# Moving the causal mask of the forgetting heads from TensorE to VectorE

## The chip, the cores and the metric

The kernel runs on one core of a Trainium2 chip. The metric is the device time of one execution in microseconds (us). The engines are called by their short names: PE is TensorE (matrix products), DVE is VectorE, ACT is ScalarE, POOL is GpSimd, and SP is SyncE, which issues most DMAs.

## The reference

One decoder layer for 512 positions of width 1024. Its first half runs two kinds of causal attention side by side on the same input, 8 heads of width 64 each, and merges them; its second half is a gated MLP with a short convolution. Only the first half matters here.

```
# forgetting attention (FoX), 8 heads
cum = cumsum(log_sigmoid(f + b_forget))
logits = q k^T / 8 + cum[t] - cum[s];  logits[s > t] = -inf
y = softmax(logits) v
# stick-breaking attention, 8 heads
z = q k^T / 8
a[t,s] = sigmoid(z[t,s]) * prod_{s<j<t} (1 - sigmoid(z[t,j]))   for s < t, else 0
y = a v
```

## The kernel before

All products keep fp32 accuracy by splitting each operand into a high part that PE takes exactly (type fp32r) and a low rest, so that one product becomes three: high with high, high with low, low with high (lines 134 to 136). Weights arrive by DMA as `raw` tiles of 128 x 1024; ACT makes the high part `wh` (line 183) and DVE the low part `wl` (line 93), a few tiles ahead of their use.

The program begins with `first_mm` (line 307), which runs the first seven column groups of the input projection and the forget logits over eight slices of the model width, while their weights and the modulation stream in. The tiles of this part lie in a pool `early`. When it is closed, the pool `att` is laid over the same memory, and a tile of `att` can be written only once the early tiles below it have been read. `att` holds the tiles that the change touches: `s2t` and `m2t`, four each, the operands of a second score product. POOL fills parts of them (lines 345 to 349).

Then come 16 heads, the 8 stick-breaking ones (`br == 1`) first and the 8 forgetting ones (`br == 0`) after. A head goes through three stages: `stage_a` computes the scores of four blocks of 128 rows into three PSUM banks and turns them into weights `pt`; `stage_b` transposes `pt` on PE and splits it; `stage_c` multiplies with the values. Between the stages of successive heads, `fill(n)` issues n products of other projections. The order on each engine is not exactly that of the text: a planner in the framework orders the instructions of PE, DVE, ACT and POOL by their place in the text and by when it expects their inputs; only SP's order is written by hand.

In `stage_a`, `scores(i)` makes two products for block i. The first (line 482) has 128 rows: high and low parts of q (`s1`) against the high part of k, twice (`m1`). The second (line 483) has 68 rows: 64 rows of high q against the low part of k, and four rows that bring in the cumulated forget logits of a forgetting head (high and low part, for t and for s). For a stick-breaking head `s2` is `s1` itself, and rows 64 to 67 of `m2` are zero. For a forgetting head `decay_rows` copies the four rows by DMA from POOL's queue. `mask(i)` (line 488) adds a triangle of -1e30 to the diagonal block of a forgetting head by a product of a bf16 identity with a bf16 triangle. Then DVE takes the negated row maximum from PSUM (line 504), and ACT the exponential with that as bias and the row sum beside it (line 505); DVE scales by the reciprocal (lines 506 and 510).

Of the kernel before, what the change touches and what calls it, by code (L numbers as in the profile page):

```python
# [8 lines left out]
F32 = mybir.dt.float32  # L9
F32R = mybir.dt.float32r  # L10
BF16 = mybir.dt.bfloat16
AF = mybir.ActivationFunctionType
ALU = mybir.AluOpType
AX = mybir.AxisListType
PSUM = bass.MemoryType.PSUM

P = 128
# [11 lines left out]
NEG = -1.0e30  # L29
# [22 lines left out]
def layer_kernel(ctx: ExitStack, tc: tile.TileContext, out, xT, x, cT, crow, wa0, wa1, bcol, bgt, w1, wct, wv, bf,  # L52
# [3 lines left out]
    V, S, G, PE = nc.vector, nc.scalar, nc.gpsimd, nc.tensor  # L56
# [15 lines left out]
    def nm(s):  # L72
        cnt[0] += 1
        return f"{s}_{cnt[0]}"

    def bank():
        return pp.tile([P, 512], F32, name=nm("ps"), tag="ps")
# [5 lines left out]
    def const(shape, dt, s):  # L83
        return cons.tile(shape, dt, name=s, tag=s)

    def fl(ap):
        return ap.bitcast(F32)
# [8 lines left out]
    def preset(shape, dt, s):  # L96
        return pre.tile(shape, dt, name=s, tag=s)
# [10 lines left out]
    ident = const([P, P], F32, "ident")  # L108
# [5 lines left out]
    make_identity(nc, ident)  # L114
    onesr = const([P, P], F32R, "onesr")
    V.tensor_copy(onesr, ones)
    identb = preset([P, P], BF16, "identb")
    V.tensor_copy(identb, ident)
    zerob = preset([P, P], BF16, "zerob")
    G.memset(zerob, 0.0)  # L120
    mska = preset([P, P], BF16, "mska")
    G.affine_select(mska, zerob, pattern=[[-1, P]], compare_op=ALU.is_ge, fill=NEG, base=0, channel_multiplier=1)
    dg = preset([P, 512], F32, "dg")
    G.memset(dg[:, 0:384], 0.0)
    G.tensor_copy(dg[:, 384:512], ident)
# [4 lines left out]
    def z(dt, s, shape=(P, 512)):  # L130
        return zp.tile(list(shape), dt, name=nm(s), tag="z", bufs=NZ)
# [14 lines left out]
    def weights(i, ahead=AHEAD):  # L146
        while state["load"] < min(len(items), i + depth[0]):
            it = items[state["load"]]
            if it[2] == 512:
                late = state.get("late")  # L150
                it[3] = late.tile([P, 512], F32, name=nm("rl"), tag="rl", bufs=4) if late else z(F32, "rs")
            else:
                it[3] = stg.tile([P, 1024], F32, name=nm("raw"), tag="raw", bufs=LOADS)
            c = 0
            for src in it[0] if isinstance(it[0], list) else [it[0]]:
                w = src.shape[-1]
                d = nc.sync.dma_start(it[3][:, c : c + w], src)
                c += w
                if depth[0] < LOADS and state["load"] >= depth[0]:
                    paced(d, reads[state["load"] - depth[0]])  # L160
            if len(it) > 5:
                G.dma_start(it[3], it[5], accum_op=ALU.add)  # L162
            state["load"] += 1
            while state["proc"] <= state["load"] - depth[0]:
                process()
        while state["proc"] < min(len(items), i + 1 + ahead):
            process()
        return items[i][4]
# [25 lines left out]
    for e in range(2):  # L194
        c = slice(e * 512, (e + 1) * 512)
# [139 lines left out]
    att = st2.enter_context(tc.tile_pool(name="att", bufs=1, reuse_waits="tile"))  # L335

    OFS = ((0, 0), (2, 0), (0, 128), (1, 0))
    SEG = (((0, 128), (128, 512)), ((0, 512),), ((0, 256),))
    ptc = [[att.tile([P, 512], F32R, name=f"ptc{i}{e}", tag=f"ptc{i}{e}") for e in range(2)] for i in range(2)]
    for e in ptc:  # L340
        for t in e:
            G.memset(fl(t[:, 0:128]), 0.0)
    s2t = [att.tile([68, 512], F32R, name=f"s2_{i}", tag=f"s2_{i}") for i in range(4)]
    m2t = [att.tile([68, 512], F32R, name=f"m2_{i}", tag=f"m2_{i}") for i in range(4)]
    for t in s2t:
        G.memset(fl(t[64:68, :]), 1.0)
        G.memset(fl(t[64:66, :]), -1.0)
    for t in m2t:
        G.memset(fl(t[64:68, :]), 0.0)
    chi = att.tile([NH, 2, 512], F32R, name="chi", tag="chi")  # L350


# [22 lines left out]
    def decay_rows(h):  # L375
        n = slot_free(idx(0, h))
        if h < 4:
            G.memset(fl(m2t[n][64:68, :]), 1.0)
        G.dma_start(s2t[n][66:68, :], chi[h : h + 1, :, :])
        G.dma_start(m2t[n][64:66, :], chi[h : h + 1, :, :])  # L380
# [9 lines left out]
    def idx(br, h):  # L390
        return h if br == 1 else NH + h
# [82 lines left out]
    def stage_a(br, h):  # L474
        d = hd[(br, h)]
        bk = [bank(), bank(), bank()]

        def scores(i):
            b, o = OFS[i]
            w = max(256, (i + 1) * P)  # L480
            tb = slice(i * P, (i + 1) * P)
            PE.matmul(bk[b][:, o : o + w], d["s1"][:, tb], d["m1"][:, 0:w], start=True, stop=False)
            PE.matmul(bk[b][:, o : o + w], d["s2"][0:68, tb], d["m2"][0:68, 0:w], start=False, stop=br == 1)  # L483

        def mask(i):
            b, o = OFS[i]
            if br == 0:
                PE.matmul(bk[b][:, o + i * P : o + i * P + P], identb, mska, start=False, stop=True)

        scores(0)  # L490
        mask(0)
        scores(2)
        scores(1)
        scores(3)
        mask(2)
        mask(1)
        mask(3)
        pt = [z(F32, "pt"), z(F32, "pt"), z(F32, "pt")]
        if br == 0:
            sm = att.tile([P, 12], F32, name=nm("sm"), tag="sm", bufs=3)  # L500
            for i in (0, 2, 1, 3):
                b, o = OFS[i]
                c = slice(o, o + (i + 1) * P)
                V.tensor_reduce(sm[:, i : i + 1], bk[b][:, c], AX.X, ALU.max, negate=True)
                S.activation(pt[b][:, c], bk[b][:, c], AF.Exp, bias=sm[:, i : i + 1], accum_out=sm[:, 4 + i : 5 + i])
            V.reciprocal(sm[:, 8:12], sm[:, 4:8])
            for i in (0, 2, 1, 3):
                b, o = OFS[i]
                c = slice(o, o + (i + 1) * P)
                V.tensor_scalar_mul(pt[b][:, c], pt[b][:, c], sm[:, 8 + i : 9 + i])  # L510
        else:
            for b in (0, 2, 1):
                w = SEG[b][-1][1]
                om = z(F32, "om")
                S.activation(om[:, 0:w], bk[b][:, 0:w], AF.Sigmoid, scale=-1.0)
                d["last"] = S.activation(pt[b][:, 0:w], bk[b][:, 0:w], AF.Sigmoid)
                G.memset(pt[b][:, SEG[b][0][1] - 1 : w : 384], 0.0)
                for s, e in SEG[b]:
                    d0 = om[:, s + 1 : e][:, ::-1]
                    V.tensor_tensor_scan(d0, d0, dg[:, 513 - (e - s) : 512][:, ::-1], 0.0, ALU.mult, ALU.max)  # L520
                    G.tensor_tensor(pt[b][:, s : e - 1], pt[b][:, s : e - 1], om[:, s + 1 : e], ALU.mult)  # L521
        d["pt"] = pt
        scored.add(idx(br, h))
        if br == 0 and h + 4 < NH:
            decay_rows(h + 4)
        if br == 1 and h >= 4 and gated:
            decay_rows(h - 4)
# [272 lines left out]
    forget_evac()  # L800
    fill(12)
    stage_a(1, 0)
    for j in range(1, NG):
        gate_after(1, j)(grp[2 + j])
    fill(18)
    stage_a(1, 1)
    fill(48)
    stage_b(1, 0)
# [3 lines left out]
    for n, (b, h) in enumerate(heads):  # L812
        f1, f2, f3 = FILL[n // 8]
        if n + 2 < 16:
            if n == 6:
                fill_to(marks["vf"])
                forget(items[vfi[0]][5])
            if n % 2 == 0:
                fill_to(marks[(n // 2 + 1, "k")])
            last = hd[heads[n + 1]].get("last")  # L820
            stage_a(*heads[n + 2])
        fill(f1)
        if n + 1 < 16:
            stage_b(*heads[n + 1])
        fill(f2)
        if n == 0:
            fill_to(marks["v1"])
            fill(9)
        stage_c(b, h)
        if n == 7:  # L830
            lim[0] = marks["y0"]
        if n == 15:
            lim[0] = len(stream)
        fill(f3)
# [158 lines left out]
    for n in range(2 * FT):  # L993
# [7 lines left out]
        if n in (23, 27):  # L1001
            t = t13[(23, 27).index(n)][:, 0:512]
# [5 lines left out]
        if n in (28, 31, 32, 35):  # L1008
            k = (28, 31, 32, 35).index(n)
            w = wdp[FP - 1][:, k * 512 : (k + 1) * 512]  # L1010
# [115 lines left out]
    for n in range(2 * FT):  # L1126
# [24 lines left out]
        t = z(F32, "cv")  # L1151
# [131 lines left out]
    for n, k in enumerate(wi):  # L1283
        w = weights(k)
        for a, p in enumerate(range(2 * n, min(FP - LATE, 2 * n + 2))):
            t = ops[p][3]
# [5 lines left out]
    for i in range(2):  # L1292
        pieces = [(1, 0, 512)] if i == 0 else [(1, 0, 256), (1, 256, 512)]
        for n, (e, c0, c1) in enumerate(pieces):
            ps = bank()[:, 0 : c1 - c0] if i else W1[0]
            for q in range(LATE):
                t = ops[FP - LATE + q][3]
# [76 lines left out]
```

## Time and profile before

| | |
|---|---|
| median of the timed runs | 745.29 us |
| the timed runs | 745.97, 744.90, 745.29 us |
| span of the profiled execution, first to last instruction | 743.3 us |
| PE busy | 732.6 us, 99% of the span |
| DVE busy | 607.5 us, 82% |
| ACT busy | 390.1 us, 52% |
| POOL busy | 81.5 us, 11% |
| stick-breaking heads, first score products | 55 to 165 us |
| forgetting heads, first score products | 179.5 to 270 us |

For the profiled execution the profile gives the span alone; the timed runs are 1.6 to 2.7 us above it.

How to read the lines: a line of the timeline has the start in the span, the duration, the engine, the line of the kernel, the operation, the tile that it writes and those it reads, and the shape; `x3` at its end means three such instructions in a row. Matmuls are pipelined, so the time that one costs is the distance between starts, not its duration. A line of the groups has the count, then the busy total in us and the mean in ns, then the idle time of the engine just before and what ended it. Score tiles of either operand appear as `m` and `s` without their numbers.

### The profile page before, as it was taken

The page shows a single profiled execution, that of the slowest core. Times are in us where ns is not written, and L with a number is a line of the kernel's source. Part 1 is how long each engine was busy: PE and PEld are TensorE (multiplying, and loading weights), DVE is VectorE, ACT ScalarE, POOL GpSimd, SP SyncE. Part 2 cuts the span into 40 slices and gives each one's busy share as a digit, 9 for nine tenths or more (in the row PEclk, how much of TensorE's full clock was granted, in tenths as well). Part 3 has the DMA queues.
Part 4 walks back from the last instruction along what each step waited for, and adds up shares of the span by engine and source line. Part 5 has one row for each costly group of instructions (what it writes and reads, how often), then busy time and mean ns, then how long its engine had stood idle before and what let it go on. Part 6 is the DMA issues. An engine that isn't in the chain of part 4 may idle for free.

```text
span 743.3 us, 9869 instructions
## 1 busy us (share of the span) xinstructions
PE 732.6 (99%) x3476; PEld 608.9 (82%) x3476; DVE 607.5 (82%) x1019; ACT 390.1 (52%) x683; POOL 81.5 (11%) x130
## 2 busy tenths in 40 slices
PE   8999999999999999999999999999999999999995
PEld 5878888888888888888889888888888888888885
DVE  6869789978788795884577889988887797679995
ACT  4567467586876564542055455444454444347550
POOL 1026223335010000000000000000001001000010
PEclk9999999999999999999999999999999999999998
DMA  8944454513422230642052787577788967646633
GB/s 325 405 178 134 151 197 144 171 57 116 170 77 96 101 127 29 228 173 85 1 214 86 227 287 230 196 225 235 253 299 228 253 199 212 212 156 228 230 82 85
DMA packets 45220, 131.95 MB, mean 178 GB/s; under 512 B 5905, under 2 KB 6417, under 8 KB 45170
## 3 DMA queue, kind: packets, MB, share of 16 engines
q1 hardware_dynamic: 38610, 113.66, 44.5%
q0 software_dynamic: 3536, 9.24, 6.4%
q10 hardware_dynamic: 3024, 8.41, 3.1%
q8 instruction: 27, 0.44, 0.2%
q14 instruction: 23, 0.19, 0.1%
HBM read 118.38 MB, written 12.85 MB: 177 GB/s over the span
## 4 chain that ended last, share of the span: by engine, by line
PE 98%; POOL 1%; DVE 1%; DMA 0%; issue 0%; DVEq 0%; POOLq 0%
PE ps L134 19%; PE ps L135 19%; PE ps L136 19%; PE ps L307 5%; PE ps L1103 5%; PE ps L1105 5%; PE ps L1104 5%; PE ps L559 3%; PE ps L541 2%; PE ps L458 2%; PE ps L457 2%; PE ps L459 2%; PE ps L900 2%; PE ps L901 2%; PE ps L902 2%; PE ps L483 1%
## 5 line engine op out<-in xcount | busy, mean ns | idle before, releaser
L183 ACT ACTIVATE wh<-raw 128x1024 fp32r<-128x1024 f32 (+1 forms) x105 | 109.2, 1042 | 109.5 <-PE ps L135 40.4
L93 DVE TENSOR_TENSOR wl<-raw,wh 128x1024 fp32r<-128x1024 f32 (+2 forms) x114 | 135.1, 1187 | 34.6 <-ACT wh L183 33.8
L134 PE MATMUL ps<-u2h,wh 128*128 128x512 f32 (+1 forms) x376 | 141.5, 376 | 0.0
L135 PE MATMUL ps<-u2l,wh 128*128 128x512 f32 (+1 forms) x376 | 141.2, 376 | 0.0
L136 PE MATMUL ps<-u2h,wl 128*128 128x512 f32 (+1 forms) x376 | 141.2, 376 | 0.0
L134 PEld LDWEIGHTS ps<-u2h,wh 128*128 128x128 f32 x376 | 70.8, 188 | 13.4 <-issue 0.6
L136 PEld LDWEIGHTS ps<-u2h,wl 128*128 128x128 f32 x376 | 70.8, 188 | 12.7
L135 PEld LDWEIGHTS ps<-u2l,wh 128*128 128x128 f32 x376 | 70.8, 188 | 12.6
L134 PE MATMUL ps<-uh,wh 128*128 128x512 f32 x200 | 79.5, 398 | 0.0
L135 PE MATMUL ps<-ul,wh 128*128 128x512 f32 x200 | 78.3, 391 | 0.0
L136 PE MATMUL ps<-uh,wl 128*128 128x512 f32 x200 | 78.1, 391 | 0.0
L1153 ACT ACTIVATE cv<-ps,cw 128x512 f32<-128x512 f32 x44 | 34.0, 773 | 42.4 <-PE ps L136 36.4
L1154 DVE SCALAR_TENSOR_TENSOR cv<-ps,cw,cv 128x511 f32<-128x511 f32 x44 | 32.8, 745 | 17.0 <-ACT cv L1153 17.0
L136 PEld LDWEIGHTS ps<-uh,wl 128*128 128x128 f32 x200 | 37.6, 188 | 8.2
L134 PEld LDWEIGHTS ps<-uh,wh 128*128 128x128 f32 x200 | 37.6, 188 | 7.3
L135 PEld LDWEIGHTS ps<-ul,wh 128*128 128x128 f32 x200 | 37.7, 188 | 7.1
L521 POOL TENSOR_TENSOR pt<-pt,om 128x127 f32<-128x127 f32 (+3 forms) x32 | 41.6, 1312 | 7.7 <-DVE om L520 7.7
L162 POOL DMA_DIRECT2D raw<-in_wdp x10 | 9.4, 942 | 249.2 <-DVE cv L1155 183.9
L1155 DVE SCALAR_TENSOR_TENSOR cv<-ps,cw,cv 128x510 f32<-128x510 f32 x44 | 32.7, 744 | 0.3
L1161 ACT ACTIVATE cv<-cv 128x512 f32<-128x512 f32 x22 | 13.9, 630 | 34.4 <-DVE cv L1155 34.4
L520 DVE TENSOR_TENSOR_SCAN om<-om,dg 128x127 f32<-128x127 f32 (+3 forms) x32 | 28.5, 946 | 0.1
L1105 PE MATMUL ps<-wh,hv 128*128 128x512 f32 x72 | 28.0, 389 | 0.0
(235 smaller groups left out, 1582.9 us busy)
## 6 DMA issues: line engine op xcount, KB each, us to landing
raw<-in_wup SPq DMA_DIRECT2D x44, 512.0 KB, 5.4
raw<-in_wa SPq DMA_DIRECT2D x32, 512.0 KB, 4.2
raw<-in_wct SPq DMA_DIRECT2D x25, 512.0 KB, 3.7
raw<-in_wdp SPq DMA_DIRECT2D x20, 512.0 KB, 5.4
wa<-in_wa SPq DMA_DIRECT2D x14, 512.0 KB, 8.1
raw<-in_wdp SPq DMA_DIRECT2D x22, 256.0 KB, 4.3
raw<-t SPq DMA_DIRECT2D x22, 256.0 KB, 3.8
raw<-in_wdp POOLq DMA_DIRECT2D x10, 512.0 KB, 7.7
```

The source lines that it names most:

```text
L93: state["read"] = V.tensor_tensor(o, i, fl(hi), ALU.subtract)
L134: PE.matmul(ps, wh, ah, start=first, stop=False)
L135: PE.matmul(ps, wh, al, start=False, stop=False)
L136: return PE.matmul(ps, wl, ah, start=False, stop=last)
L183: state["hi"] = S.activation(h[:, 0:cols], r[:, 0:cols], AF.Copy)
L307: PE.matmul(grp[g], w, u, start=j == 0 and n == 0, stop=j == KT - 1 and n == (1 if g == 7 else 2))
L521: G.tensor_tensor(pt[b][:, s : e - 1], pt[b][:, s : e - 1], om[:, s + 1 : e], ALU.mult)
L1103: PE.matmul(ps, ah, bh, start=first, stop=False, skip_group_check=onto)
L1104: PE.matmul(ps, ah, bl, start=False, stop=False, skip_group_check=onto)
L1105: return PE.matmul(ps, al, bh, start=False, stop=last, skip_group_check=onto)
L1153: S.activation(t, ps, AF.Identity, bias=cw[:, n, 3:4], scale=cw[:, n, 2:3])
L1154: V.scalar_tensor_tensor(t[:, 1:], ps[:, 0:511], cw[:, n, 1:2], t[:, 1:], ALU.mult, ALU.add)
```

## The change

The bf16 identity, the bf16 triangle and the products with them go. A mask of 128 x 512 in fp32 takes their place: zeros, with the triangle in its last 128 columns, so that a slice that ends at column 512 fits a block of any width. For a forgetting head DVE reads the scores from PSUM and the mask from SBUF in one instruction, writes the negated sum to `pt` in SBUF, and keeps the row minimum; ACT's exponential reads that and works in place with scale -1. The four row blocks are scored in the order 0, 2, 1, 3 for both kinds of heads, as before.

The second score product takes all 128 rows. For that `s2t` and `m2t` have 128 rows, and POOL zeroes rows 64 to 127: one fill more for each tile of `s2t`, a larger one for each of `m2t`.

```diff
-    identb = preset([P, P], BF16, "identb")
-    V.tensor_copy(identb, ident)
-    zerob = preset([P, P], BF16, "zerob")
-    G.memset(zerob, 0.0)
-    mska = preset([P, P], BF16, "mska")
-    G.affine_select(mska, zerob, pattern=[[-1, P]], compare_op=ALU.is_ge, fill=NEG, base=0, channel_multiplier=1)
+    mska = preset([P, 512], F32, "mska")
+    G.memset(mska, 0.0)
+    tri = mska[:, 384:512]
+    G.affine_select(tri, tri, pattern=[[-1, P]], compare_op=ALU.is_ge, fill=NEG, base=0, channel_multiplier=1)
...
-    s2t = [att.tile([68, 512], F32R, name=f"s2_{i}", tag=f"s2_{i}") for i in range(4)]
-    m2t = [att.tile([68, 512], F32R, name=f"m2_{i}", tag=f"m2_{i}") for i in range(4)]
+    s2t = [att.tile([P, 512], F32R, name=f"s2_{i}", tag=f"s2_{i}") for i in range(4)]
+    m2t = [att.tile([P, 512], F32R, name=f"m2_{i}", tag=f"m2_{i}") for i in range(4)]
     for t in s2t:
+        G.memset(fl(t[64:128, :]), 0.0)
         G.memset(fl(t[64:68, :]), 1.0)
         G.memset(fl(t[64:66, :]), -1.0)
     for t in m2t:
-        G.memset(fl(t[64:68, :]), 0.0)
+        G.memset(fl(t[64:128, :]), 0.0)
...
-            PE.matmul(bk[b][:, o : o + w], d["s2"][0:68, tb], d["m2"][0:68, 0:w], start=False, stop=br == 1)
-
-        def mask(i):
-            b, o = OFS[i]
-            if br == 0:
-                PE.matmul(bk[b][:, o + i * P : o + i * P + P], identb, mska, start=False, stop=True)
-
-        scores(0)
-        mask(0)
-        scores(2)
-        scores(1)
-        scores(3)
-        mask(2)
-        mask(1)
-        mask(3)
+            PE.matmul(bk[b][:, o : o + w], d["s2"][:, tb], d["m2"][:, 0:w], start=False, stop=True)
+
+        for i in (0, 2, 1, 3):
+            scores(i)
...
-                V.tensor_reduce(sm[:, i : i + 1], bk[b][:, c], AX.X, ALU.max, negate=True)
-                S.activation(pt[b][:, c], bk[b][:, c], AF.Exp, bias=sm[:, i : i + 1], accum_out=sm[:, 4 + i : 5 + i])
+                n, m = pt[b][:, c], mska[:, (3 - i) * P : 512]
+                V.tensor_tensor_reduce(n, bk[b][:, c], m, -1.0, -NEG, ALU.add, ALU.min, sm[:, i : i + 1])
+                S.activation(n, n, AF.Exp, scale=-1.0, bias=sm[:, i : i + 1], accum_out=sm[:, 4 + i : 5 + i])
```

## The prediction

> **What bounds the kernel now.** I read the page first: busy shares, then the chain of work that ended last.
>
> ```profile
> span 743.3 us, 9869 instructions
> ...
> PE 732.6 (99%) x3476; PEld 608.9 (82%) x3476; DVE 607.5 (82%) x1019; ACT 390.1 (52%) x683; POOL 81.5 (11%) x130
> ...
> PE 98%; POOL 1%; DVE 1%; DMA 0%; issue 0%; DVEq 0%; POOLq 0%
> ```
>
> TensorE (PE) is busy 99% of the span and makes up 98% of the chain. The view of waits, for PE alone, says that almost nothing ever holds it up:
>
> ```profile
> PE ps L196 <- DMA cbr<-in_crow: 2.4, 1, 2.4
> PE ps L483 <- POOL m L349: 0.2, 1, 0.2
> ```
>
> One wait is the start of the program. The other is a second score product (line 483) that waits for a fill by GpSimd (POOL, line 349). So a microsecond of PE issue time saved or added moves the end by a microsecond; work on VectorE (DVE), ScalarE (ACT) and POOL counts only where it makes PE wait. POOL's 1% of the chain is that one place, and the change edits it.
>
> Times below are set against the profiled span of 743.3 us. The timed runs are 744.90 to 745.97 with a median of 745.29, so about 2.0 us lie around the span; I add the changes to the median.
>
> **Term 1: the masks leave PE.** The timeline of PE at a forgetting head, from its first score product to the second product of the work that follows:
>
> ```profile
> 179.51 0.28 PE L482 MATMUL ps<-m,s 128*128 128x256 f32 x1
> ...
> 179.75 0.23 PE L488 MATMUL ps<-mska,identb 128*128 128x128 bf16 x1
> ...
> 180.94 0.34 PE L488 MATMUL ps<-mska,identb 128*128 128x128 bf16 x3
> ...
> 181.41 0.39 PE L135 MATMUL ps<-ul,wh 128*128 128x512 f32 x1
> ```
>
> A stick-breaking head issues the same eight score products in the same order and has no masks, so it is the changed head already measured:
>
> ```profile
> 117.78 0.28 PE L482 MATMUL ps<-m,s 128*128 128x256 f32 x1
> 117.90 0.29 PE L483 MATMUL ps<-m,s 68*128 68x256 f32 x1
> 118.02 0.34 PE L482 MATMUL ps<-m,s 128*128 128x384 f32 x1
> ...
> 119.33 0.40 PE L135 MATMUL ps<-ul,wh 128*128 128x512 f32 x1
> ```
>
> The stretch is 181.41 - 179.51 = 1.90 us with masks and 119.33 - 117.78 = 1.55 us without: 0.35 us a head. The mean duration in the grouped row would mislead, because pipelined products overlap:
>
> ```profile
> L488 PE MATMUL ps<-mska,identb 128*128 128x128 bf16 x32 | 4.6, 225 | 0.0
> ```
>
> 32 products are 8 heads of 4. By starts they cost 8 x 0.35 = 2.8 us, not 4.6 (8 x 4 x 0.225 would be 7.2). All of it is on the path, so term 1 is **-2.8 us**.
>
> [...]
>
> **Term 2: 128 rows instead of 68.** In the rows above the 128-row product starts at 117.78, the 68-row one at 117.90, the next at 118.02: 0.12 us each at 256 columns. Rows cost PE nothing; term 2 is **0**. I see nothing that would make it a gain.
>
> **Term 3: the fills that the 128 rows need.** This one can bite. Each of the four s2 tiles gets one more fill (rows 64 to 127); those of the m2 tiles only grow in rows. POOL cannot start them until the early weights' space is free, and the first head waits for the end of this queue. The timeline of all engines there:
>
> ```profile
> 48.42 0.69 DVE L93 TENSOR_TENSOR ul<-xt,uh 128x512 fp32r<-128x512 f32 x1 [2.90 <-ACT xt L279]
> ...
> 48.69 0.39 PE L307 MATMUL ps<-uh,wh 128*128 128x512 f32 x1
> 48.92 0.39 PE L307 MATMUL ps<-uh,wl 128*128 128x512 f32 x1
> ...
> 49.17 0.97 PE L307 MATMUL ps<-ul,wh 128*128 128x512 f32 x3
> ...
> 51.21 0.99 POOL L346 MEMSET s<- 4x512 f32 x2
> ...
> 54.92 1.91 POOL L349 MEMSET m<- 4x512 f32 x4
> 54.97 0.28 PE L482 MATMUL ps<-m,s 128*128 128x256 f32 x1
> ...
> 55.49 0.39 PE L483 MATMUL ps<-m,s 68*128 68x256 f32 x1 [0.24 <-POOL m L349]
> ...
> 57.02 0.40 PE L135 MATMUL ps<-ul,wh 128*128 128x512 f32 x1
> ```
>
> Eight fills start between 51.21 and 54.92, so a fill of 512 columns takes (54.92 - 51.21) / 8 = 0.46 us. Those of 2 and of 4 rows step alike, and I take the same for 64. Four more put the first m2 fill 4 x 0.46 = 1.86 us later. Already this head takes 57.02 - 54.97 = 2.05 us where the undisturbed one took 1.55: PE loses 0.5 us here today. If PE's order stays, it would lose 0.5 + 1.86 = 2.36 us, and term 3 is +1.86.
>
> But PE's order need not stay. The program's instructions are ordered by a planner that pulls ready work ahead of work it expects to wait. The rows show it: line 307 is written as (wh with uh, wl with uh, wh with ul) for each column group, yet PE ran the ul products of the first groups together at 49.17, behind a run of uh products, and ul was ready at 48.42 + 0.69 = 49.11. So the planner's idea of PE, ACT and DVE is within 0.1 us of the chip here. Its idea of POOL was too fast by at least the 0.5 us lost, or it would have moved products ahead of line 483 already. With four more fills it may see the wait and put other products first, of this head or of the projection in progress, which needs nothing from POOL. Then only what it underestimates remains.
>
> The ends for term 3 are therefore -0.5 (it pulls enough that today's loss goes too) and +1.86 (it sees nothing). I take **+0.9**, half of the four fills: a planner near the chip on three engines is unlikely to be blind to the whole of 1.86 us, and unlikely to cover all, since it misses 0.5 us now.
>
> **Term 4: the VectorE pass.** 32 row maxima become 32 passes that add the mask, write the sum and keep its minimum. The new instruction is not in this trace. Rows by shape, between 175 and 275 us, and one scan from the whole run:
>
> ```profile
> L504 DVE TENSOR_REDUCE sm<-ps 128x1 f32<-128x512 f32 x8 | 5.4, 680 | 0.0
> L93 DVE TENSOR_TENSOR pl<-ps,ph 128x512 fp32r<-128x512 f32 x7 | 4.8, 685 | 0.8 <-ACT ph L90 0.8
> L504 DVE TENSOR_REDUCE sm<-ps 128x1 f32<-128x384 f32 x8 | 4.4, 547 | 0.0
> L504 DVE TENSOR_REDUCE sm<-ps 128x1 f32<-128x256 f32 x8 | 3.3, 414 | 0.0
> L504 DVE TENSOR_REDUCE sm<-ps 128x1 f32<-128x128 f32 x8 | 2.3, 288 | 3.3 <-PE ps L488 3.3
> L203 DVE DVE_READ_ACCUMULATOR raw<-raw,cbc 128x1 f32 x8 | 0.6, 80 | 0.0
> ```
>
> ```profile
> L520 DVE TENSOR_TENSOR_SCAN om<-om,dg 128x511 f32<-128x511 f32 x8 | 13.1, 1637 | 0.0
> ```
>
> The maxima total 5.4 + 4.4 + 3.3 + 2.3 = 15.4 us. A two-operand pass with one operand in PSUM takes 685 against 680 ns; with an accumulator read-out of 80 ns, the likely case (the nearest rows) is +0.085 x 32 = 2.7 us. The low end is no change or a little less. The high end is the scan's ratio, 1637 / 680 = 2.4, on all of them: +21.7 us. What covers it:
>
> ```profile
> 180.00:276.00 96.00, 96.00 (x514) 80.56 (x514) 81.61 (x159) 65.65 (x143) 4.13 (x8) 1.00 0.32 114
> ```
>
> ```profile
> 185.14 1.22 DVE L93 TENSOR_TENSOR wl<-raw,wh 128x1024 fp32r<-128x1024 f32 x1
> ```
>
> ```profile
> 194.34 0.39 PE L136 MATMUL ps<-uh,wl 128*128 128x512 f32 x1
> ```
>
> In the forgetting stretch (third busy column) DVE is busy 81.6 of 96 us, 14.4 idle. And it works ahead: counting the weight splits in order, the low half that DVE finished at 185.14 + 1.22 = 186.36 is first used by PE at 194.34, 8.0 us later, the shortest such lead that I count in the stretch. So DVE may fall 14.4 + 8.0 = 22.4 us behind before PE waits; 2.7 lies well inside, and the high end just inside. Term 4 is **0**, for both ends.
>
> **Edits with one answer.** ACT's exponentials now read SBUF and work in place: ACT has 96 - 65.65 = 30 us to spare. The score banks are given back after DVE's pass instead of after the exponential, and PE never waited for a bank. The larger mask is filled in the first microseconds on POOL, long before a head uses it, and dropping the bf16 identity takes a short DVE copy away while PE does its warm-up products. POOL's later copies of the decay rows wait for a head's last score product as before. No DMA is added or moved; the queue of SP keeps its order.
>
> **Sum.** -2.8 + 0 + 0.9 + 0 = -1.9 us: 745.29 - 1.9 = **743.4 us**.
>
> **Rivals.**
> - *PE's order stays.* Term 3 is the full +1.86: 745.29 - 2.8 + 1.86 = 744.35. For it: the order today already runs into the wait. Chance 0.30.
> - *The wait vanishes,* because the planner pulls enough ahead or places the m2 fills before the s2 fills: between 745.29 - 2.8 = 742.5 and, with today's 0.5 gone, 742.0. Against it: POOL runs these fills in written order today. Chance 0.10.
> - *The wait slows the clock: slower than before.* When PE stops at the end of the run, the windows of the timeline show the granted clock (third figure from the right) fall:
>
> ```profile
> 734.94 0.28 PE L1105 MATMUL ps<-wdh,hv 128*128 128x256 f32 x1
> ```
>
> ```profile
> 736.00:738.00 2.00, 0.00 (x0) 0.85 0.30 113
> 738.00:740.00 2.00, 0.00 (x0) 0.50 0.02 7
> ```
>
> ```profile
> 6.16 4.34 PE ps L199 x10
> ```
>
> PE ended at 735.22. A mean of 0.85 with an end value of 0.50 puts the fall at 737.4, 2.2 us after PE stopped: shorter than a full wait of 2.36 us, so such a wait could trip it. A slow stretch like the start's, where ten 512-column products took 4.34 us (0.434 each, against 48.92 - 48.69 = 0.23 above), loses 4.34 x (1 - 0.23 / 0.434) = 2.0 us: 744.35 + 2.0 = 746.4. It needs the full 1.86 of term 3; below a wait of some 2.2 us it cannot happen. Chance 0.06. [...]
> - *DVE becomes the bound.* From 0.70 us more for each of the 32 passes (22.4 / 32) PE would wait; at 1.0 us more it loses 32 - 22.4 = 9.6 us: 745.29 - 1.9 + 9.6 = 753. No row is that slow. Chance 0.04.
>
> **How the numbers follow.** The forecast's case, a wait partly covered, has chance 0.50 and spreads from 742.5 to 744.35. A measurement of this kernel tells changes over about 0.2%, 1.5 us. Faster means below 743.8: some 0.7 of the forecast's case and the vanished wait, 0.35 + 0.10 = 0.45. Within: the rest of that case, the kept order and the slow clock, 0.15 + 0.30 + 0.06, less 0.05 for a loss that no row points to: 0.46. Slower: the DVE case and that loss, 0.09. The range runs from the vanished wait, 742.0, to the kept order with 0.85 us of spread between runs, 745.2; the slow clock and the DVE case stay outside.
>
> **What would show it.** Right: no bf16 products; a forgetting head at 1.55 us between the same two points; POOL with twelve fills before the first m2 fill, which ends near 57.3 us; at the first head either a PE wait of up to 2.4 us, or products of line 134 to 136 (or other scores) between lines 482 and 483; PE waits elsewhere still nil; DVE some 3 us busier between 180 and 276. Wrong: a PE wait on DVE in the forgetting heads; a granted clock below 1 near 60 us; fills of 64 rows that take another time than those of 4; a different order of PE's work elsewhere.

## The result, and the profile after

| | before | after |
|---|---|---|
| median of the timed runs | 745.86 us | 742.03 us |
| lowest and highest | 744.90 to 745.97 | 740.91 to 743.61 |
| ratio, with 95% interval | | 0.9957, 0.9945 to 0.9969 |
| span of the profiled execution | 743.3 us | 741.8 us |

(Five runs of each; the three of before known at the prediction are among them.) Three single executions in the series of this document ran for 1234 to 2960 us and are left out of all ratios; one of them was the profiled one of the first series with 15 products ahead, so nothing is read from that trace. The change makes the kernel 3.2 us faster by the ratio, 2.3 to 4.1 by its interval: outside the 0.2% that I had set, on the faster side. The forecast was 743.4, so it went the right way and was too small by 1.4 us. The execution of the changed kernel that was profiled was the slowest of its five, 743.61 us.

The page of the changed kernel: its span, the busy line and the chain by engine.

```profile
span 741.8 us, 9838 instructions
...
PE 730.3 (98%) x3444; PEld 608.1 (82%) x3444; DVE 608.6 (82%) x1050; ACT 390.5 (53%) x683; POOL 83.1 (11%) x134
...
PE 92%; DVE 4%; ACT 2%; DMA 1%; issue 1%; DVEq 0%; ACTq 0%
```

PE has 32 instructions fewer and is still the bound. The 4% of DVE in the chain are not the new pass. They come with one wait, which the view of waits for PE names beside the wait at the start:

```profile
PE ps L194 <- DMA cbr<-in_crow: 2.5, 1, 2.5
PE ps L548 <- DVE vv L93: 0.7, 1, 0.7
```

Line 548 is a head's product with the values. It stands at 99 us, far from the forgetting heads, and the chain in front of it goes back over DVE and ACT to a load of weights that took 6.76 us:

```profile
79.73 6.76 DMA raw<-in_wct
```

None of the other profiles has this wait, so I count it to that execution and not to the change.

A forgetting head after, PE's timeline from the first score product on:

```profile
208.63 0.28 PE L481 MATMUL ps<-m,s 128*128 128x256 f32 x1
208.75 0.28 PE L482 MATMUL ps<-m,s 128*128 128x256 f32 x1
208.86 0.34 PE L481 MATMUL ps<-m,s 128*128 128x384 f32 x1
...
209.91 0.39 PE L132 MATMUL ps<-uh,wh 128*128 128x512 f32 x1
210.14 0.40 PE L133 MATMUL ps<-ul,wh 128*128 128x512 f32 x1
```

No bf16 products are left; 210.14 - 208.63 = 1.51 us where it was 1.90, and 0.04 less than the 1.55 of a head that never had masks. That 0.04 comes back below.

The first head, with PE, PE's weight loads (PEld) and POOL:

```profile
52.01 0.99 POOL L344 MEMSET s<- 64x512 f32 x2
52.94 0.98 POOL L345 MEMSET s<- 4x512 f32 x2
...
55.79 0.77 PE L481 MATMUL ps<-m,s 128*128 128x256 f32 x2
...
56.40 0.39 PE L132 MATMUL ps<-uh,wh 128*128 128x512 f32 x1
...
56.88 0.19 PEld L481 LDWEIGHTS ps<-m,s 128*128 128x128 f32 x1 [0.41 <-DVE fq L356]
56.88 0.50 PE L481 MATMUL ps<-m,s 128*128 128x512 f32 x1
...
57.22 0.39 PE L133 MATMUL ps<-ul,wh 128*128 128x512 f32 x1
...
57.55 1.91 POOL L348 MEMSET m<- 64x512 f32 x4
...
58.15 0.39 PE L134 MATMUL ps<-uh,wl 128*128 128x512 f32 x1
...
58.38 0.28 PE L482 MATMUL ps<-m,s 128*128 128x256 f32 x1
```

Twelve fills stand before the first m2 fill, as many as counted, and a fill of 64 rows takes what one of 4 rows takes. The m2 fills begin 57.55 - 52.01 = 5.54 us after the s2 fills, which is 12 x 0.46; the queue itself began 0.8 us later in this execution than in that of before. PE does not wait for the fills. The planner put two further first products of the head and six products of the projection (lines 132 to 134) in front of the first second product.

Two of the moved score products are late for another reason. The second of the pair at 55.79 starts 0.41 us behind the first, where 0.11 is usual, and the one at 56.88 starts 0.26 us later than the usual 0.23 behind its neighbour. Each writes to a PSUM bank of its own. The line above names the second of these banks: it holds the forget logits, which DVE is still reading (`fq`). For the other bank, the view of waits of the same kernel's repeat, up to 60 us, names DVE's last read of the k projection (`m`); that this is about the bank follows from the kernel, where the pair differs only in the rows of q and in the bank:

```profile
PE ps L481 <- DVE m L93: 0.2, 1, 0.2
```

The next lines are the new pass on DVE, by shape, between 175 and 275 us, and the forgetting stretch (third busy column: DVE):

```profile
L493 DVE CUSTOM_DVE_ANT_0 pt<-ps,mska 128x512 f32<-128x512 f32 x8 | 5.5, 684 | 0.0
L493 DVE DVE_READ_ACCUMULATOR2_ANT sm<- 128x1 f32 x32 | 2.6, 82 | 0.0
```

```profile
180.00:276.00 96.00, 96.00 (x499) 82.14 (x498) 81.61 (x189) 68.50 (x146) 4.12 (x8) 1.00 0.34 120
```

### The profile page after: what moved, and what is told of

Read it like the earlier page. It is cut to its first block, busy times and chain, and to the rows that moved or that the text cites. A ratio compares the mean times of both kernels' runs of the same rounds, so it can differ in the third digit from the quotient of the medians.

```text
span 741.8 us, 9838 instructions
## 1 busy us (share of the span) xinstructions
PE 730.3 (98%) x3444; PEld 608.1 (82%) x3444; DVE 608.6 (82%) x1050; ACT 390.5 (53%) x683; POOL 83.1 (11%) x134
## 4 chain that ended last, share of the span: by engine, by line
PE 92%; DVE 4%; ACT 2%; DMA 1%; issue 1%; DVEq 0%; ACTq 0%
PE ps L134 18%; PE ps L133 18%; PE ps L132 18%; PE ps L305 5%; PE ps L1092 5%; PE ps L1094 5%; PE ps L1093 5%; PE ps L548 3%; PE ps L530 2%; PE ps L890 2%; PE ps L889 2%; PE ps L891 2%; DVE om L509 1%; PE ps L481 1%; PE ps L482 1%
## 5 line engine op out<-in xcount | busy, mean ns | idle before, releaser
L181 ACT ACTIVATE wh<-raw 128x1024 fp32r<-128x1024 f32 (+1 forms) x105 | 109.2, 1042 | 108.8 <-PE ps L133 36.3
```

What stands on the lines that cost most here:

```text
L181: state["hi"] = S.activation(h[:, 0:cols], r[:, 0:cols], AF.Copy)
```

## The experiments

Start times of heads tell parts of a microsecond that medians can't. This table has, for the profiled executions, the distance in us between the first score products of two successive heads: the first two heads, two stick-breaking ones (the fourth and fifth), two forgetting ones (the eleventh and twelfth).

| kernel | first two | stick-breaking | forgetting | median of runs | ratio to before |
|---|---|---|---|---|---|
| before | 5.95 | 15.17 | 12.34 | 745.3 to 745.9 | 1 |
| masks only (68 rows) | 5.89 | 15.17 | 11.99 | 742.61 | 0.9963 (0.995 to 0.9977) |
| rows only (masks on PE) | 6.15 | 15.10 | 12.31 | 745.48 | 0.9999 (0.999 to 1.0008) |
| rows only, again | 6.13 | 15.10 | 12.31 | 745.47 | 1.0001 (0.9992 to 1.001) |
| changed kernel | 6.12 | 15.10 | 11.92 | 742.03 | 0.9957 (0.9945 to 0.9969) |
| changed kernel, again | 6.15 | 15.10 | 11.92 | 741.86 | 0.9958 (0.9945 to 0.997) |
| m2 fills first | 5.77 | 15.10 | 11.92 | 742.13 | 0.9954 (0.9942 to 0.9967) |
| m2 fills first, 15 products ahead | | | | 741.47 | 0.9946 (0.9932 to 0.9959) |
| the same, again | 4.70 | 15.10 | 11.92 | 741.35 | 0.9948 (0.9934 to 0.9962) |
| order kept | 9.34 | 15.10 | 11.92 | 744.65 | 0.9989 (0.9978 to 1.0001) |
| 64 rows in the first head | 6.96 | 15.10 | 11.92 | 743.11 | 0.9968 (0.9956 to 0.998) |

(In the version with 15 products ahead one group of three, 0.68 us, has moved in front of the first head, so its 4.70 stands for 5.38 in the others.)

**Masks alone.** The changed kernel with the old fills and 68 rows.

```diff
-    s2t = [att.tile([P, 512], F32R, name=f"s2_{i}", tag=f"s2_{i}") for i in range(4)]
+    s2t = [att.tile([68, 512], F32R, name=f"s2_{i}", tag=f"s2_{i}") for i in range(4)]
...
-        G.memset(fl(t[64:128, :]), 0.0)
...
-            PE.matmul(bk[b][:, o : o + w], d["s2"][:, tb], d["m2"][:, 0:w], start=False, stop=True)
+            PE.matmul(bk[b][:, o : o + w], d["s2"][0:68, tb], d["m2"][0:68, 0:w], start=False, stop=True)
```

> The masks go to DVE, but the second score product keeps its 68 rows and the tiles their old fills. Theory A (the 128 rows themselves save PE time, some 0.067 us a head over all 16 heads, 1.1 us together, beside the masks' 2.85 us and a first head that costs 0.2 us more): 2.85 us under the kernel before, ratio about 0.9962, a forgetting head 0.36 us shorter between its first score product and the fifth product behind it, a stick-breaking head as before (2.24 us), and 0.5 us lost at the first head as before. Rival B (rows cost nothing; the whole gain is the masks): as fast as the changed kernel in rows of the trace, every head at 2.20 us.

Measured: 742.61, 2.76 us under the median of before in the same series (745.37). Each forgetting head is 12.34 - 11.99 = 0.35 us shorter, as forecast, and eight of them make 2.8 us. From a head's first score product to the fifth product behind it, heads of both kinds take 2242 ns here, as the stick-breaking heads of before, and 2202 in the changed kernel: the 0.04 us belong to the rows, as Theory A has it. The old stall at the first head is still there:

```profile
PE ps L481 <- POOL m L347: 0.2, 1, 0.2
```

**Rows alone.** The kernel before with 128 rows and the new fills; the masks stay on PE.

```diff
...
-            PE.matmul(bk[b][:, o : o + w], d["s2"][0:68, tb], d["m2"][0:68, 0:w], start=False, stop=br == 1)
+            PE.matmul(bk[b][:, o : o + w], d["s2"][:, tb], d["m2"][:, 0:w], start=False, stop=br == 1)
```

> The masks stay on PE as bf16 products; the second score product takes 128 rows with the new fills. Theory A: 16 x 0.067 = 1.1 us saved and 0.2 us more at the first head, so 0.9 us under the kernel before, ratio about 0.9988; a stick-breaking head at 2.20 us instead of 2.24 up to the fifth product behind it. Rival B: no gain from rows and 0.2 to 1.9 us lost at the first head by the four fills, so 0.2 to 1.9 us slower than before.

Measured: no change in the time. Yet rows are not free of effect on PE: every stick-breaking head is 0.067 us shorter (15.17 to 15.10), every forgetting head with masks 0.03. Against that stand 0.2 us more at the first head and 0.07 between the last stick-breaking and the first forgetting head, so some 0.35 us are left by the heads, and this profile lost them again in the MLP, where PE waited for DVE's convolutions:

```profile
PE ps L134 <- DVE cv L1156: 0.9, 2, 0.5
```

My 0.9 had counted 0.067 us for the forgetting heads too, where only 0.03 shows as long as their masks are on PE, and had left out the 0.07 between the two kinds.

> 128 rows and their fills with the masks still on PE, once more. In its first profile PE had gained 0.78 us by the last head and lost 1.5 us again at 447 and 453 us, in the MLP, waiting for VectorE's convolutions behind a late weight. Theory A (a matter of the single execution): PE is 0.8 us early at the last head again, and no such wait or one of another size; time 744.5 if the timed runs are spared, 745.4 if they are not. Rival B (it belongs to this kernel's timing): the same two waits at the same two places, of 0.5 us or so each, and 745.4 again.

Measured: 745.47, and no wait in the MLP. So that wait belongs to the execution. PE gained 0.55 us between the second head and the last, as in the first profile (0.52), but came 0.4 us later to the first head, so it was not 0.8 us early at the last one: the start of an execution can differ by more than that (first score product at 54.5 and 55.4 us in these two). Rows alone are worth a few tenths of a microsecond, which the timed runs don't resolve.

**The m2 fills first.** The changed kernel with two loops exchanged.

```diff
+    for t in m2t:
+        G.memset(fl(t[64:128, :]), 0.0)
     for t in s2t:
         ...
-    for t in m2t:
-        G.memset(fl(t[64:128, :]), 0.0)
```

> The changed kernel with the fills of the m2 tiles written ahead of those of the s2 tiles, so that the first head's fill ends some 5 us sooner. Theory A: the first two heads lie 5.40 us apart as an undisturbed pair would, 0.7 us less than in the changed kernel (6.12 us), PE runs the score products in written order without a wait, and the time is 0.7 us under the changed kernel's. Rival C (the lost time at the first head is not the fills but the bank that still holds the forget logits): the loss stays at 0.3 us or more, and the gain is under 0.4 us.

Measured: 742.13, the same time as the changed kernel. PE's products stay in written order and no fill is waited for, but the first head still takes 0.39 us more than the others, and the timeline says for what:

```profile
55.88 0.74 DVE L356 SCALAR_TENSOR_TENSOR fq<-ps,bfs,fq 8x512 f32<-8x512 f32 x1
...
56.67 0.19 PEld L481 LDWEIGHTS ps<-m,s 128*128 128x128 f32 x1 [0.32 <-DVE fq L356]
56.68 0.50 PE L481 MATMUL ps<-m,s 128*128 128x512 f32 x1
```

So Rival C is right. The head's last bank still holds the forget logits, which DVE reads until 56.62. In the kernel before DVE had done the same read by 56.05 and the head wanted that bank at 56.31: the stall on the fills had covered it.

**The changed kernel once more**, on the chip of these runs.

> The changed kernel once more, on the chip of the three others. Theory A: 3.2 to 3.8 us under the kernel before, ratio 0.995 to 0.9957, so that the gains of the masks alone and of the rows alone add up to it (2.85 + 0.9 = 3.75). Rival B: the sum of the two parts falls short of it by a microsecond or more.

Measured: 741.86, 3.5 us under the median of before in this series, as Theory A has it. By the ratios the two parts (0.37% and 0.01%) fall 0.04%, 0.3 us, short of the whole, which is less than the intervals. PE is 3.4 us earlier than before at the last head and only 1.6 at the end: 1.8 us were given back around 447 and 453 us, in this profile alone of the changed kernel's two.

```profile
434.85 2.54 SPq L155 DMA_DIRECT2D raw<-in_wup  x2
...
440.48 1.06 ACT L181 ACTIVATE wh<-raw 128x1024 fp32r<-128x1024 f32 x1 [6.05 <-DMA raw<-in_wup]
...
445.20 0.47 PE L132 MATMUL ps<-u2h,wh 128*128 128x512 f32 x1 [1.07 <-DVE cv L1144]
```

ACT waits 6.05 us for a weight of the MLP; the convolution behind it in ACT's queue comes late, and with it the bank that PE wants. Between 435 and 440 us the DMA share of this trace is 1.01, with 257 GB/s, so the DMA engines were busy all the time. Why this load is late in some executions I did not settle.

**The order kept.** The changed kernel with the first head's score products held in written order and the projection behind them: what the rival "PE's order stays" would have been. (`put` makes the two score products of one block.)

```diff
...
+            if (br, h) != (1, 0):
+                put()
+            elif not kept:
+                kept.append(put())
+            else:
+                with tc.issue_after(kept[-1].ins):
+                    kept.append(put())
...
-    fill(18)
+    with tc.issue_after(kept[-1].ins):
+        fill(18)
```

> The changed kernel with the eight score products of the first head held in their written order, and the products of the projection held behind them; all else as changed, so that the wait of the four further fills stands bare. Theory A (the planner's products covered the wait, and the fills are as long as forecast): PE waits at the first line of second products for 2.0 to 2.4 us, the distance from the first score product of the first head to that of the second grows from 6.12 us in the changed kernel to 7.6 to 7.8 (5.37 undisturbed and some 2.3 of wait), and the time is 743.4 to 743.8 against 742.0. Rival B (the fills never cost much: what holds the head is the bank in which the forget logits lie): no more than 6.3 us between the heads, time as the changed kernel's. Rival D (such a wait lowers the clock): the granted clock of PE falls below 1 behind the wait, and the time is 745 to 746.

Measured: 744.65, between the times of A and D, and 9.34 us between the first two heads, more than A's 7.6 to 7.8. PE waits as long as forecast, and the clock falls after it (windows: PE busy first, third figure from the right the granted clock):

```profile
55.40 0.28 PE L484 MATMUL ps<-m,s 128*128 128x256 f32 x1
57.75 0.38 PE L485 MATMUL ps<-m,s 128*128 128x256 f32 x1 [2.07 <-POOL m L348]
...
59.03 0.62 PE L132 MATMUL ps<-uh,wh 128*128 128x512 f32 x1
59.45 0.63 PE L133 MATMUL ps<-ul,wh 128*128 128x512 f32 x1
```

```profile
57.70:59.00 1.30, 1.25 (x7) 1.19 (x8) 1.01 (x1) 0.47 (x1) 1.30 (x3) 1.00 0.35 63
59.00:62.40 3.40, 3.40 (x9) 2.64 (x8) 3.24 (x4) 3.40 (x9) 2.76 (x6) 0.50 0.82 273
```

The head's products up to the next work take 3.63 us where 1.28 is undisturbed: a wait of 2.35 us, against 0.5 + 1.86 = 2.36 forecast. Then, 1.3 us after PE has work again, the clock is 0.50 for 3.4 us, and products step by 0.42 instead of 0.23 us. 9.34 - 5.38 - 2.35 leaves 1.6 us for it.

The mean granted clock tells two kinds of executions apart. Seven of the twelve have 0.993 or 0.994, as the one with the trace (0.994), where all 25 of before in this series have 0.996 to 0.998; these seven average 745.4 us, the time of D. The other five, at 0.996 to 0.998, average 743.7, the time of A. Only one of the seven has a trace.

In two other traces the clock fell after different lengths of idle time of PE. In the kernel before PE stopped at 735.22, at the end of the run, and the clock fell at 737.4, 2.2 us later. In the changed kernel PE stops at 733.78, the clock holds at 1.00 and falls at 739.03, 5.2 us later:

```profile
732.21:735.61 3.40, 1.57 (x14) 1.37 (x12) 3.01 (x8) 0.29 (x1) 0.00 (x0) 1.00 0.42 157
735.63:739.02 3.39, 0.00 (x0) 0.00 (x0) 2.78 (x9) 0.00 (x0) 0.00 (x0) 1.00 0.15 56
```

What decides whether a wait of 2.07 us is followed by a fall, as here, or by none, as the clocks of the other five executions have it, these traces do not show. The rivals "PE's order stays" and "the wait slows the clock" are thus two outcomes of one kernel. The planner's moved products spared both: 9.34 - 6.12 = 3.2 us on PE in the profiled execution, 2.6 us by the medians.

**64 and 96 rows.** The changed kernel with second products over 64 rows in stick-breaking heads and 96 in forgetting heads.

```diff
...
-            PE.matmul(bk[b][:, o : o + w], d["s2"][:, tb], d["m2"][:, 0:w], start=False, stop=True)
+            n = 64 if br == 1 else 96
+            PE.matmul(bk[b][:, o : o + w], d["s2"][0:n, tb], d["m2"][0:n, 0:w], start=False, stop=True)
```

> The changed kernel with second products over 64 rows in the eight stick-breaking heads and over 96 in the eight forgetting heads; fills as in the changed kernel. A head's stretch from its first score product to the fifth product behind it was 2242 ns with 68 rows and 2202 with 128. Theory A (any product over fewer than 128 rows makes the products behind it start a few ns later): 2242 in both kinds of heads, PE loses some 0.067 us a head again. Rival B (by the rows left idle): 2245 with 64 rows, 2223 with 96. Rival C (68 alone is odd, its last 4 rows): 2202 in both. In the first head, 64 rows need no fill at all: if the fills alone held that head, the distance from its first score product to that of the second head falls from 6.12 to some 5.4 us; if the bank of the forget logits held it, it stays above 5.7. Time: 742.3 by A with the first head free (742.0 + 1.1 - 0.7), 743.1 by A without that, 741.3 by C with the first head free.

Measured: 753.98, ratio 1.0114 (1.0099 to 1.0129): 12 us slower than the changed kernel, which none of the theories had. The heads with 96 rows take 2242 ns, as those with 68, so the loss does not go by the rows left idle (Rival B had 2223). The ones with 64 rows take 3764:

```profile
123.97 0.28 PE L481 MATMUL ps<-m,s 128*128 128x256 f32 x1
124.17 0.38 PE L483 MATMUL ps<-m,s 64*128 64x256 f32 x1
124.49 0.44 PE L481 MATMUL ps<-m,s 128*128 128x384 f32 x1
124.86 0.44 PE L483 MATMUL ps<-m,s 64*128 64x384 f32 x1
125.22 0.38 PE L481 MATMUL ps<-m,s 128*128 128x256 f32 x1
```

The step from a 64-row product of 256 columns to the next is 0.32 us, where it is 0.12 with 68 or 128 rows. From the second to the eighth, a head's steps between 128 rows and 64 are about 0.2 us longer than in the changed kernel (0.31 to 0.43 us against 0.12 to 0.23); the first step and the one behind the eighth are 0.1 longer. A head has eight products and loses 3764 - 2202 = 1.56 us, and eight heads would make 12.5 us. Why the step is longer the trace does not show.

**64 rows in the first head alone**, so that it needs no fill.

```diff
...
+            n = 64 if (br, h) == (1, 0) else P
...
```

> The changed kernel with 64 rows in the second products of the first head alone, which so needs no fill; 128 rows everywhere else. Theory A (the fills hold the first head): no wait and no products pulled into it, 5.4 us from its first score product to the second head's instead of 6.12, time 741.3 against 742.0 and below the kernel with masks alone. Rival B (the bank that holds the forget logits holds the first head as well): 0.3 to 0.5 us of the stall stay, 5.7 to 5.9 us, time 741.7.

Measured: 743.11, with 6.96 us between the first two heads; both expectations fell to the same cost, since that head takes 3764 ns as well. No wait of PE is left but the one at the start, so the head was free of its fills and paid 6.96 - 5.38 = 1.58 us for it. A head so much longer also reaches its last bank later, so this run cannot tell A from B.

**DVE's pass twice and three times.** The repeats write the same numbers again.

```diff
                 V.tensor_tensor_reduce(n, bk[b][:, c], m, -1.0, -NEG, ALU.add, ALU.min, sm[:, i : i + 1])
+                V.tensor_tensor_reduce(n, bk[b][:, c], m, -1.0, -NEG, ALU.add, ALU.min, sm[:, i : i + 1])
```

> The changed kernel with the VectorE pass of the forgetting heads done twice, the second writing the same numbers over the first. A head's four passes take 684 + 551 + 419 + 284 ns and four read-outs of 82: 2.27 us, so VectorE gets 18.1 us more over eight heads. PE's order is that of the changed kernel. Theory A (the cover of 14.4 us idle and 8.0 us of lead holds): VectorE is busy some 18 us more between 180 and 276 us, no wait of PE on VectorE there, time as the changed kernel's within 0.5 us. Rival B (the cover is smaller, since VectorE's lead in weights is all that counts inside one head): waits of PE on VectorE's weight halves or sums in the forgetting heads, of 5 us and more, time over 746.

Measured: 742.73, ratio 0.9969 (0.9959 to 0.9979), 0.7 us over the changed kernel by the medians, with intervals that overlap. PE waits once on DVE in the forgetting heads, and that head takes 0.45 us longer:

```profile
PE ps L482 <- DVE m L93: 0.2, 1, 0.2
```

The busy line of its page:

```profile
PE 730.0 (98%) x3444; PEld 607.6 (82%) x3444; DVE 620.8 (84%) x1114; ACT 390.7 (53%) x683; POOL 83.1 (11%) x134
```

DVE got 620.8 - 608.6 = 12.2 us busier, not 18.1. I had added durations; DVE's instructions overlap as PE's do, and the cost goes by starts:

```profile
211.24 0.55 DVE L493 CUSTOM_DVE_ANT_0 pt<-ps,mska 128x384 f32<-128x384 f32 x1
211.72 0.08 DVE L493 DVE_READ_ACCUMULATOR2_ANT sm<- 128x1 f32 x1
211.72 0.42 DVE L493 CUSTOM_DVE_ANT_0 pt<-ps,mska 128x256 f32<-128x256 f32 x1
```

These lines are from the timeline of the changed kernel. A pass of 384 columns steps by 0.48 us with its read-out inside, not 0.55 + 0.08. So this run tried 12.2 us. That is less than the 14.4 us of idle time, and yet one head waited: idle time summed over the stretch does not cover a need inside one head.

> The changed kernel with the VectorE pass of the forgetting heads done three times, the later ones writing the same numbers over the first: 36.3 us more on VectorE over eight heads, where twice gave 18.1 and 0.45 us of PE waits. Theory A (the cover is 14.4 us idle and 8.0 us of lead, together 22.4): PE waits on VectorE for some 36.3 - 22.4 = 13.9 us in the forgetting heads, 742 + 13.9 = 756 us; 750 to 757, since the planner moves some projection products into the gaps. Rival B (the cover is larger, since work that VectorE has not done by the end of the stretch is caught up behind it): waits under 5 us, time under 747.

Measured: 750.23, ratio 1.0072 (1.0058 to 1.0086), 8.2 us over the changed kernel. The four longest waits of PE behind the start, from its view of waits (two shorter ones make 0.6 us):

```profile
PE ps L134 <- DVE wl L93: 1.7, 2, 1.4
PE ps L550 <- ACT ph L90: 1.3, 1, 1.3
PE ps L132 <- DVE m L93: 1.3, 1, 1.3
PE ps L132 <- DVE sm L495: 0.5, 1, 0.5
```

DVE is 24.2 us busier in all (632.8). PE ends 5.5 us later than in the changed kernel's profile, and the medians differ by 8.2, so 16 to 19 us of the 24.2 were covered: DVE does hold PE up, and before the 22.4 us of the estimate. Only 1.7 us of these waits are for the low weights `wl`, whose lead the estimate had counted; 1.8 us end with a read of PSUM by DVE (`m` and `sm`), so with a bank given back, and 1.3 with a tile from ACT. The time lies at the low edge of Theory A's, by two errors that offset each other: 36.3 us of work that was 24.2, and a cover that was smaller than 22.4.

**A version meant to lose nothing at the first head:** the m2 fills first, and one more group of the projection ahead of the head.

```diff
...
-    fill(12)
+    fill(15)
     stage_a(1, 0)
...
-    fill(18)
+    fill(15)
     stage_a(1, 1)
```

> The changed kernel with the m2 fills ahead of the s2 fills, and three projection products (one group) that stood behind the first head's score products put ahead of them; a version meant to lose nothing at the first head. With the m2 fills first alone, the first head kept a stretch of 2593 ns where 2202 is undisturbed, and the trace named the bank of the forget logits, still read by VectorE when the head's last score products wanted it. Theory A (that bank holds it): with 0.68 us more ahead of the head the stretch is 2202 ns, PE ends 0.4 us earlier than with the m2 fills first alone, and against masks alone all 16 heads are 0.067 us shorter and the first one loses no 0.5: 742.6 - 1.07 - 0.5 = 741.1 us. Rival B (the bank is held by something that moves with the head): the stretch stays near 2.6 us and the time near 742.0.

> The version meant to lose nothing at the first head (m2 fills ahead of the s2 fills, one more group of projection products ahead of the head's score products), once more, since the execution profiled before was disturbed and tells nothing of the first head. Theory A (the bank of the forget logits held it): first head's stretch 2202 ns, no wait of PE before the MLP, 5.37 us to the second head, median 741.1 to 741.5. Rival B: the stretch stays near 2.6 us.

Measured: 741.47 and 741.35. The first head now looks like any other:

```profile
55.69 0.28 PE L481 MATMUL ps<-m,s 128*128 128x256 f32 x1
55.80 0.28 PE L482 MATMUL ps<-m,s 128*128 128x256 f32 x1
...
56.96 0.39 PE L132 MATMUL ps<-uh,wh 128*128 128x512 f32 x1
57.19 0.40 PE L133 MATMUL ps<-ul,wh 128*128 128x512 f32 x1
```

56.96 - 55.69 = 1.27 us, 2202 ns to the fifth product behind, and no wait of PE after the start. The changed kernel lost 6.12 - 5.38 = 0.74 us at this head, about half at each of the two banks, and here that is gone. It is the fastest of the kernels by its medians, but the intervals of the ratios overlap with the changed kernel's; the gain over it is shown by the trace, not by the times.

## Why the prediction was right, and where it was off

In the repeat's trace the heads of the changed kernel add up to -3.4 us on PE against before: -2.8 for the masks, -0.8 for the rows, +0.2 at the first head. The ratio says -3.2. The prediction had -1.9: terms 2 and 3 were off by 0.8 and 0.7 us, both to the same side. The range held by luck. Its low end of 742.0 stood for a wait that vanishes and for rows that gain nothing; the first series, 742.03, lies 0.03 us inside it, and the repeat, 741.86, outside.

- *Term 1, the masks, -2.8:* right, 0.35 us a head in the trace and 2.76 us in the run with the masks alone. Pricing them by a stretch of the timeline against that of a head without masks held: 0.35 / 4 = 88 ns a mask.
- *Term 2, the rows, 0:* this step failed twice. "Rows cost PE nothing; I see nothing that would make it a gain" was read from two starts at 256 columns. It overlooked what comes behind: over the next dozen products PE runs a few ns slower after 68-row products than after 128-row ones (behind 68 rows, steps of up to 240 ns for a dozen products where 227 is usual; behind 128 rows, up to 236 for five; 2242 against 2202 ns from the head's start to the fifth product, 0.067 us by the next head). Over the heads, less the 0.07 us lost between the two kinds, that is some 0.9 us, and the traces show 0.8. Why the rows do this stays open. And the sentence does not hold for fewer rows: 64 cost 1.56 us a head.
- *Term 3, the fills, +0.9:* right in mechanism, mis-sized, +0.2. The bare wait would have been 2.35 us, so the +1.86 of four fills at 0.46 was exact. The guess of "half of the four fills" was too high: the planner moved eight products, and no wait on POOL is left. What remains at this head is 0.74 us at two banks that DVE still reads, which the prediction did not look for ("PE never waited for a bank"); against the 0.5 lost before, that is the +0.2. The moved products reach these banks sooner. In written order with the m2 fills first, the bank of the forget logits alone costs 0.39.
- *Term 4, the pass on DVE, 0:* right, with a working that counted too much. The pass takes 684 ns and the read-out 82, as the nearest rows said, but they overlap. By starts the pass takes 12 ns more than the maximum that it replaces (610 against 598 at 512 columns), 0.4 us in all 32. DVE is as busy between 180 and 276 us as before, 81.61 us in both, and 1.1 us busier over the whole span, where 3 us more were announced. The cover of 22.4 us was too large: 16 to 19 by the run with three passes.
- *Rivals:* the kept order costs the 1.86 given to it in five executions (743.7 us on average) and 1.7 us more in seven (745.4), whose mean clock of 0.993 or 0.994 goes with the fall to 0.50 in the one trace. "Below a wait of some 2.2 us it cannot happen" was read from one end of a run. In the changed kernel the clock fell 5.2 us after PE's last product, and in the kept order a wait of 2.07 us was enough once. DVE as the bound is real, and nearer than its price said (0.5 to 0.6 us more a pass instead of 0.7).

## What to carry to other kernels

Before pricing an edit on a busy engine by a repeated shape, compare whole stretches up to the next like point, not two starts: the cost or gain can lie in what follows. Put a bare wait in the sum only after asking whether a planner that knows of it has other work to put there; when it has none, price the clock's fall too, as a chance (here a wait of 2.07 us brought one that cost 1.6 us). A stall that one resource explains may hide a second one behind it, so free both before counting it as gained.

## What the runs showed of the hardware that I had not expected

- Products over 64 rows between products over 128 step by 0.32 us instead of 0.12 at 256 columns; those over 68 and 96 rows don't.
- With 68- or 96-row products in place of 128-row ones, 0.04 us were lost by the fifth product behind (2242 against 2202 ns); with 68 rows, where the products behind step slower for longer, 0.067 in all (15.17 against 15.10 us).
- 2.07 us without work halved the granted clock for 3.4 us, starting 1.3 us after the work had come back. At the end of a run the clock fell 2.2 us after PE's last product in the kernel before and 5.2 us after it in the changed one.
- A fill on POOL of 64 rows and 512 columns takes as long as one of 2 rows, 0.46 us.
- Two executions of one kernel differed by 0.9 us (rows alone) and by 1.2 us (changed kernel) at the first head already, and a late weight in the MLP cost 1.8 us in one, which is as much as the smaller effects here.
